# Two units of eight products instead of four ahead of the first block's seven-product units, and a place of its own for one token sum of the second block

## The chip, the cores and the metric

The kernel runs on one core of one Trainium2 chip. The metric is the device time of one execution in microseconds (us), the median of three runs.

## What is computed

A decoder trunk of one layer over 16 meta tokens and 512 real tokens, width 1024: a gated feed-forward block, a token mixer (two kinds of attention with gated branches), and a second gated feed-forward block. Cut to what the change touches:

```python
def swiglu(h, w_in, w_out):
    gu = h @ w_in
    gate, up = jnp.split(gu, 2, axis=-1)
    return (jax.nn.silu(gate) * up) @ w_out

h = h + 0.5 * swiglu(rms_norm(h, ffn1_norm[l]), ffn1_w_in[l], ffn1_w_out[l])
h = h + token_mixer(rms_norm(h, mix_norm[l]), ...)
h = h + 0.5 * swiglu(rms_norm(h, ffn2_norm[l]), ffn2_w_in[l], ffn2_w_out[l])
```

D_FF is 2816, so `w_in` has 2 x 22 column groups of 128: 22 **units** `u`, each a gate group and an up group.

## The kernel before, in words

Every matrix product is made of float32 operands split into a high part (`hi`, L130, a cast on ScalarE, called ACT in the rows) and a rest (`lo`, L137 or L139, a subtraction on VectorE, DVE); a product of 128 features is three matmuls on TensorE, PE (L275, L276, L278 in `prod`).

**Two kinds of unit.** The features of the input (1024) are halved into 2 x 512 and the tokens into two halves, which gives blocks A11, A12 (first token half) and A21, A22. A *plain* unit (`Units.plain`) makes all eight block products: per gate and up, two token halves and two feature halves, each 4 x 3 = 12 matmuls, 96 in all. A *seven* unit (`Units.seven`, called by `Units.unit`) takes gate and up together as a 2 x 2 block product by Winograd's form with seven products, 84 matmuls, out of A11, A12, A22 and four token sums S1 to S4 (`Halves.sums`, built by `Halves.diff`, L398, and split by `parts`).

**Weights.** A plain unit takes two pieces of 128x1024, each loaded with one DMA (L236) and split once. A seven unit takes four pieces, A, B, C and D: A is landed in two halves on the queue of SyncE, SP (L191), and a third DMA adds to its second half while it lands (`add`, L195, issued on the queue of GpSimd, POOL); C is landed and added to in the same way, D is landed; B is made of C and D by two additions on DVE (L217, L218) in a tile `tc`, of which there is one. A, B and C are split at 1024 columns, D at 512 into a tile `wD`. There are three buffers each for `raw`, `wh` and `wl`, two each for `rawC` and `rawD`. `piece()` hands out a piece, splits up to three ahead and loads up to five ahead.

**Order.** `NC = (4, 3)` is the number of plain units with which the first and the second block begin. `ffn_pieces` lists the weights accordingly, and `early` weaves the steps of the plain units with the entry of the second token half and the four token sums; the loops after it run the seven units from `NC` on. In the first block the entry belongs to this: `enter_first` and `enter_rest` bring in the tokens (squares on ACT, `entry_rms` on DVE, then a power operation on POOL, L319, in `rsq`; then `entry_scale` on DVE, L623), and `enter_second` transposes the second token half on PE (L631) and splits A21 and A22. The plain units need all four blocks.

The program's text does not fix the order on the engines: a planner orders the instructions of each engine by its own estimate of when their operands are there, and lets a later one go ahead where an earlier one is not ready; only where the code asks for it (`issue_after`, `inline`) is the order kept. Each engine and each queue then works strictly in that order, and an instruction that waits holds up all behind it. A DMA issued on POOL waits on POOL's queue like any other instruction.

In the second block the sums S3, S1, S2 and S4 get their places from `places2` (in this order: `tc`, `own`, `tc`, and `own` again), and `acts_tile2(1)` is the tile for the activations of units 2 and 3.

Of the kernel before, what the change touches and what calls it, by code (L numbers as in the profile page):

```python
# [11 lines left out]
F32 = mybir.dt.float32  # L12
# [22 lines left out]
KG1 = [(0, 4), (4, 3), (7, 4)]  # L35
KG2 = [(0, 4), (4, 4), (8, 3)]
NU = DFF // P
NC = (4, 3)
TH = T // 2


# [38 lines left out]
def kernel(  # L80
# [32 lines left out]
    def nm(s):  # L113
        nid[0] += 1
        return f"{s}_{nid[0]}"
# [35 lines left out]
    def ffn_pieces(wi, wo, second):  # L151
        nc_ = NC[second]
        for j0, n in KG2 if second else KG1:
            for i, u in enumerate(in_turns(j0, n)):
                if 2 * j0 + i < nc_:
                    pieces.extend([("w", [(wi[u], 8, 128)]), ("w", [(wi[NU + u], 8, 128)])])
                else:
                    seven_pieces(wi[u], wi[NU + u], 4)
            if second:
                for m in range(0, KD, 2):  # L160
                    cut = lambda m: wo[m // 4][:, 2 * j0 : 2 * (j0 + n), P * (m % 4) : P * (m % 4) + P]
                    seven_pieces(cut(m), cut(m + 1), n)
            else:
                for m in range(0, KD, 2):
                    seven_pieces(*(wo[m + b][:, 2 * j0 : 2 * (j0 + n)] for b in range(2)), n)
# [573 lines left out]
    def early(X, ff, dsts, second, sums, more, alone=0):  # L739


        u = [ff.plain(d, i == 0 and not alone) for i, d in enumerate(dsts)]
        main = u[0][:4] + u[1][:2]
        if alone:
            main[1:1] = [enter_rest]
        run(main[:alone] + second[:3] + main[alone:] + second[3:] if alone else weave(main, second))
        run(weave(u[0][4:] + [s for v in ([u[1][2:]] + u[2:]) for s in v], sums + more))
# [96 lines left out]
    ]  # L844
    early(X, ff1, [act1(u) for u in range(NC[0])], second, X.sums(), [nothing], 6)
    def rest_of(m):

        hi(xH[:, m], hT[:, m], gmT[:, m : m + 1])
        lo(xL[:, m], hT[:, m], xH[:, m], gmT[:, m : m + 1])
        if m == 0:  # L850
            A.activation(sqacc, hT[:, m], AF.Square)
        else:
            sq = ff1.new("u", 2, 2)
            A.activation(sq, hT[:, m], AF.Square)
            (V if m > 5 else G).tensor_tensor(out=sqacc, in0=sqacc, in1=sq, op=ALU.add)
        A.dma_start(h1d[:, m], hT[:, m, M:])
        G.tensor_copy(xm[:, m, 0:M], xH[:, m, :M].bitcast(F32))
        i = G.tensor_copy(xm[:, m, 32 : 32 + M], xL[:, m, :M].bitcast(F32))
        shared["xm"] = getattr(i, "ins", i)
# [22 lines left out]
    for gi, (j0, n) in enumerate(KG1):  # L882
        for u in range(max(2 * j0, NC[0]), 2 * (j0 + n)):
            does = (lambda f, *v: lambda: [f(i) for i in v])
# [652 lines left out]
    for hf in range(2):  # L1537
        c = slice(S // 2 * hf, S // 2 * (hf + 1))
# [20 lines left out]
    def acts_tile2(i):  # L1559

        if i == 2:
            t = kp.tile([P, KD, S], F32, tag="o", name=nm("acts2")).bitcast(F32R).rearrange("p k c -> p (k c)")
        else:
            t = ap2.tile([P, 7 * S], F32R, tag=f"acts{i}", name=nm("acts2"), bufs=1)
        return t[:, : 7 * S].rearrange("p (b a c) -> p b a c", b=2, a=7)

    def places2():
        own = ap2.tile([P, 2 * S], F32, tag="own", name="own", bufs=1)
        new_tc = lambda: ap2.tile([P, PW], F32, tag="tc", name=nm("tc"), bufs=1)
        return [new_tc, lambda: own, new_tc]  # L1570

    X2.new_places = places2
    X2.a21 = lambda: acts_tile2(3)
# [9 lines left out]
    ]  # L1583
    early(X2, ff2, [act2(u) for u in range(NC[1])], second, [nothing] + X2.sums(), [])
    stage = {}
# [17 lines left out]
    for gi, (j0, n) in enumerate(KG2):  # L1603
        for u in range(max(2 * j0, NC[1]), 2 * (j0 + n)):
            ff2.unit(act2(u), u == 2 * (j0 + n) - 1)
# [77 lines left out]
```

## Time and profile before

| | us |
|---|---|
| median of three runs | 1091.29 (1090.96 to 1091.56) |
| the profiled execution | 1090.99 |
| its span, first to last instruction | 1089.2 |
| PE busy in the span | 1079.7 |
| DVE busy | 851.2 |
| ACT busy | 612.6 |
| POOL busy | 177.5 |

Of the profiled execution 1090.99 - 1089.2 = 1.8 us lie around the span. A busy share is a mean over stages with different limits. PE's matmuls are pipelined, so that what one costs is read from the distance between two starts, not from its own duration.

### The profile page before, as it was taken

What the parts mean: (1) busy time and instruction counts of PE and PEld (TensorE: products, weight loads), DVE (VectorE), ACT (ScalarE), POOL (GpSimd) and SP (SyncE); (2) the same over time, 40 slices, a digit from 0 to 9 for tenths busy, and PEclk for the clock granted to TensorE, in tenths of its full rate; (3) what the DMA queues carried; (4) which work ended last, traced back from release to release, by engine and by line L of the source; (5) the groups of instructions that cost most, each with busy time, mean ns of one, the idle gap of its engine ahead of it and who ended that gap; (6) DMA issues with size and microseconds to landing.
All of it is one profiled execution on the core that took longest, in us unless ns stands there. A gap on an engine that the chain in (4) does not pass through costs nothing.

```text
span 1089.2 us, 21633 instructions
## 1 busy us (share of the span) xinstructions
PE 1079.7 (99%) x8407; PEld 1035.8 (95%) x8407; DVE 851.2 (78%) x1616; ACT 612.6 (56%) x1143; POOL 177.5 (16%) x209
## 2 busy tenths in 40 slices
PE   8999999999999999999999999999999999999998
PEld 7999999999999999999887888899999999999998
DVE  7868868988889577788787655578898778887895
ACT  7556456656666455456555633355476466645664
POOL 1011111112124431122100000000122211221120
PEclk9999999999999999999999999999999999999999
DMA  8478787688776323112211224456588877887753
GB/s 274 128 192 190 179 197 197 151 220 215 178 178 172 120 81 117 57 42 80 79 59 58 78 78 138 153 180 188 141 198 178 201 188 180 177 199 186 166 123 102
DMA packets 107111, 163.84 MB, mean 150 GB/s; under 512 B 10288, under 2 KB 57648, under 8 KB 107008
## 3 DMA queue, kind: packets, MB, share of 16 engines
q1 hardware_dynamic: 71440, 119.67, 34.6%
q0 software_dynamic: 25888, 31.02, 19.2%
q10 hardware_dynamic: 9680, 11.77, 3.4%
q8 instruction: 66, 1.08, 0.4%
q14 instruction: 37, 0.30, 0.1%
HBM read 158.19 MB, written 6.32 MB: 151 GB/s over the span
## 4 chain that ended last, share of the span: by engine, by line
PE 90%; DVE 5%; ACT 2%; DMA 2%; issue 1%; POOL 0%; ACTq 0%; SPq 0%; DVEq 0%
PE ps L275 15%; PE ps L276 15%; PE ps L278 15%; PE pt L275 12%; PE pt L276 12%; PE pt L278 12%; DVE wl L137 1%; DMA raw<-in_w2i_dram 1%; ACT wh L130 1%; ACT t L1140 1%; PE pt L1225 0%; PE pt L1180 0%; DMA raw<-in_w1i_dram 0%; DMA xt<-in_x_dram 0%; PE ps L1347 0%
## 5 line engine op out<-in xcount | busy, mean ns | idle before, releaser
L276 PE MATMUL ps<-x,wh 128*128 128x264 f32 (+2 forms) x768 | 224.6, 293 | 0.8 <-DVE x L139 0.4
L275 PE MATMUL ps<-x,wh 128*128 128x264 f32 (+2 forms) x768 | 225.1, 293 | 0.1
L278 PE MATMUL ps<-x,wl 128*128 128x264 f32 (+2 forms) x768 | 224.1, 292 | 0.0
L130 ACT CAST wh<-raw 128x1024 fp32r<-128x1024 f32 (+3 forms) x134 | 137.8, 1030 | 125.7 <-PE ps L276 50.1
L137 DVE TENSOR_TENSOR wl<-raw,wh 128x1024 fp32r<-128x1024 f32 (+3 forms) x134 | 161.1, 1203 | 54.1 <-ACT wh L130 51.4
L276 PEld LDWEIGHTS ps<-x,wh 128*128 128x128 f32 x768 | 144.6, 188 | 3.7 <-DVE x L139 0.9
L275 PEld LDWEIGHTS ps<-x,wh 128*128 128x128 f32 x768 | 144.8, 189 | 3.3 <-ACT hT L650 0.3
L278 PEld LDWEIGHTS ps<-x,wl 128*128 128x128 f32 x768 | 144.7, 188 | 2.8
L275 PE MATMUL pt<-x,wh 128*128 128x264 f32 (+2 forms) x416 | 125.4, 301 | 0.0
L276 PE MATMUL pt<-x,wh 128*128 128x264 f32 (+2 forms) x416 | 124.9, 300 | 0.0
L278 PE MATMUL pt<-x,wl 128*128 128x264 f32 (+2 forms) x416 | 124.6, 300 | 0.0
L275 PE MATMUL ps<-acts,wh 128*128 128x264 f32 (+1 forms) x352 | 100.4, 285 | 0.1
L278 PE MATMUL ps<-acts,wl 128*128 128x264 f32 (+1 forms) x352 | 99.6, 283 | 0.0
L276 PE MATMUL ps<-acts,wh 128*128 128x264 f32 (+1 forms) x352 | 99.5, 283 | 0.0
L137 DVE TENSOR_TENSOR wl<-tc,wh 128x1024 fp32r<-128x1024 f32 (+1 forms) x61 | 72.4, 1188 | 33.1 <-ACT wh L130 32.9
L130 ACT CAST wh<-tc 128x1024 fp32r<-128x1024 f32 (+1 forms) x61 | 62.3, 1021 | 58.7 <-DVE tc L218 47.2
L278 PEld LDWEIGHTS pt<-x,wl 128*128 128x128 f32 x416 | 78.5, 189 | 2.8
L275 PEld LDWEIGHTS pt<-x,wh 128*128 128x128 f32 x416 | 78.4, 188 | 2.9 <-issue 0.3
L276 PEld LDWEIGHTS pt<-x,wh 128*128 128x128 f32 x416 | 78.2, 188 | 2.5
L137 DVE TENSOR_TENSOR wl<-rawC,wh 128x1024 fp32r<-128x1024 f32 (+1 forms) x61 | 73.1, 1199 | 5.7 <-ACT wh L130 5.4
L130 ACT CAST wh<-rawC 128x1024 fp32r<-128x1024 f32 (+1 forms) x61 | 62.2, 1020 | 25.5 <-PE pt L276 19.2
L275 PEld LDWEIGHTS ps<-acts,wh 128*128 128x128 f32 x352 | 66.4, 189 | 0.7 <-DVE h2T L877 0.3
(368 smaller groups left out, 3065.8 us busy)
## 6 DMA issues: line engine op xcount, KB each, us to landing
rawC<-in_w2i_dram SPq DMA_DIRECT2D x19, 512.0 KB, 4.4
raw<-in_w2i_dram SPq DMA_DIRECT2D x38, 256.0 KB, 3.3
rawC<-in_w1i_dram SPq DMA_DIRECT2D x18, 512.0 KB, 4.5
raw<-in_w1i_dram SPq DMA_DIRECT2D x36, 256.0 KB, 3.4
raw<-in_wm_dram SPq DMA_DIRECT2D x18, 512.0 KB, 4.5
raw<-in_wg_dram SPq DMA_DIRECT2D x16, 512.0 KB, 3.4
raw<-in_wout_dram SPq DMA_DIRECT2D x16, 512.0 KB, 3.4
rawD<-in_w2i_dram SPq DMA_DIRECT2D x19, 256.0 KB, 3.8
```

The costliest lines, as they stand in the source:

```text
L130: return A.copy(o, i)
L137: return V.tensor_tensor(out=o, in0=i, in1=h, op=ALU.subtract)
L275: PE.matmul(ps, sH, mH, start=first, stop=False, **more)
L276: PE.matmul(ps, sH, mL, start=False, stop=False, **more)
L278: shared["mm"] = PE.matmul(ps, sL, mH, start=False, stop=last, **more)
L1140: A.activation(t, t, AF.Exp, bias=nmx, scale=-1.0, accum_out=l[:, j : j + 1])
```

## The change

`NC` becomes (2, 3): units 2 and 3 of the first block are seven units. Their weights are loaded and combined like those of the other seven units, and the token sums are woven into two plain units. In the second block the third sum to be built, S2, no longer gets the shared tile `tc` but the first 1024 float32 columns of the tile for the activations of units 2 and 3.

```diff
-NC = (4, 3)
+NC = (2, 3)
...
     def places2():
         own = ap2.tile([P, 2 * S], F32, tag="own", name="own", bufs=1)
         new_tc = lambda: ap2.tile([P, PW], F32, tag="tc", name=nm("tc"), bufs=1)
-        return [new_tc, lambda: own, new_tc]
+
+        pair = acts_tile2(1).rearrange("p b a c -> p (b a c)").bitcast(F32)
+        return [new_tc, lambda: own, lambda: pair]
```

## Rows read from the trace of the kernel before

**Rows 1.** The page's head: busy us of the engines, share of the span, instructions.
```profile
PE 1079.7 (99%) x8407; PEld 1035.8 (95%) x8407; DVE 851.2 (78%) x1616; ACT 612.6 (56%) x1143; POOL 177.5 (16%) x209
```
**Rows 2.** Busy time by stretch: us, PE, PEld, DVE, ACT, POOL, clock, DMA share, GB/s.
```profile
25.50:40.20 14.70, 14.70 (x121) 14.70 (x121) 14.37 (x19) 9.21 (x16) 0.00 (x0) 1.00 0.28 95
40.20:51.90 11.70, 11.70 (x98) 11.70 (x97) 8.59 (x14) 5.16 (x9) 1.74 (x2) 1.00 0.55 136
51.90:63.60 11.70, 11.70 (x98) 11.70 (x97) 5.38 (x8) 3.19 (x5) 1.70 (x2) 1.00 0.67 161
```
**Rows 3.** PE in order of time: the first matmuls of units 2, 3 and 4.
```profile
40.23 0.28 PE L275 MATMUL ps<-x,wh 128*128 128x264 f32 x1
...
51.93 0.29 PE L275 MATMUL ps<-x,wh 128*128 128x264 f32 x1
...
63.60 0.28 PE L275 MATMUL ps<-x,wh 128*128 128x264 f32 x1
```
**Rows 4.** DVE in order of time: splits of S2 and S4, first addition of B.
```profile
40.28 1.25 DVE L137 TENSOR_TENSOR x<-acts,x 128x1056 fp32r<-128x1056 f32 x1
...
44.23 1.25 DVE L137 TENSOR_TENSOR x<-acts,x 128x1056 fp32r<-128x1056 f32 x1
...
54.62 0.69 DVE L217 TENSOR_TENSOR tc<-rawC,rawD 128x512 f32<-128x512 f32 x1
```
**Rows 5.** POOL in order of time, 15 to 20 us.
```profile
15.48 1.05 POOL L195 DMA_DIRECT2D rawC<-in_w1i_dram  x1 [6.29 <-DMA rawC<-in_w1i_dram]
16.72 0.87 POOL L195 DMA_DIRECT2D rawC<-in_w1i_dram  x1 [0.19 <-issue]
19.39 0.71 POOL L319 TENSOR_TENSOR rin<-rin,nhalf 128x2 f32<-128x2 f32 x1 [1.80 <-DVE rin L613]
```
**Rows 6.** SP's queue in order of time: issues at 7 and 15 us.
```profile
7.09 1.34 SPq L191 DMA_DIRECT2D rawC<-in_w1i_dram  x2
...
15.08 0.33 SPq L236 DMA_DIRECT2D raw<-in_w1i_dram  x1
```
**Rows 7.** Tile `raw`, 15.0 to 15.2 us: landing of the issue at 15.08.
```profile
DMA to landing us min/median/max: 5.3/5.3/5.3
```
**Rows 8.** Tile `raw`, 17.0 to 17.3 us: landing of the issue at 17.17.
```profile
DMA to landing us min/median/max: 7.0/7.0/7.0
```
**Rows 9.** Tile `raw`, 0 to 70 us: shortest, median and longest landing.
```profile
DMA to landing us min/median/max: 2.6/4.4/8.7
```
**Rows 10.** DVE, then PE, in order of time, 13 to 21 us.
```profile
13.82 1.23 DVE L137 TENSOR_TENSOR wl<-raw,wh 128x1024 fp32r<-128x1024 f32 x1
...
15.92 1.22 DVE L137 TENSOR_TENSOR wl<-raw,wh 128x1024 fp32r<-128x1024 f32 x1
...
19.13 0.17 DVE L613 TENSOR_SCALAR rin<-rin 128x2 f32<-128x2 f32 x1 [0.76 <-ACT sq L598]
20.14 1.42 DVE L623 TENSOR_SCALAR xt<-xt,rin 128x1024 f32<-128x1024 f32 x2 [0.83 <-DMA raw<-in_w1i_dram]
...
21.04 0.30 PE L631 MATMUL pt<-ident,xt 128*128 128x128 f32 x1 [0.63 <-DVE xt L623]
```
**Rows 11.** Second block, DVE in order of time: split of B, S2, S4.
```profile
779.67 1.23 DVE L137 TENSOR_TENSOR wl<-tc,wh 128x1024 fp32r<-128x1024 f32 x1 [0.53 <-ACT wh L130]
780.93 1.23 DVE L398 TENSOR_TENSOR tc<-own,x 128x1024 f32<-128x1024 f32 x1
...
783.54 1.22 DVE L137 TENSOR_TENSOR x<-tc,x 128x1024 fp32r<-128x1024 f32 x1
```
**Rows 12.** Second block, PE in order of time, and the stretch around it.
```profile
784.25 0.28 PE L276 MATMUL pt<-x,wh 128*128 128x256 f32 x1
784.82 0.38 PE L276 MATMUL ps<-x,wh 128*128 128x256 f32 x1 [0.28 <-DVE x L137]
...
780.00:790.00 10.00, 9.72 (x83) 9.52 (x82) 9.93 (x13) 6.19 (x11) 0.79 (x1) 1.00 0.42 95
```

## What the change was predicted to do

> **What bounds the kernel now.** I read the page's head first, then the busy time by stretch, then PE, DVE, POOL and SP in order of time. PE is busy in 1079.7 of 1089.2 us [rows 1], and in the stretch that the change touches it never rests: from 25.50 us (first product with the second token half) to 63.60 (first seven unit) all of every stretch is PE time [rows 2]. So a matmul that is left out there is worth its full distance, as long as PE's operands keep coming. DVE is the engine to watch: 14.37 of 14.70 us in the stretch up to 40.20, then 8.59 and 5.38 of 11.70 while units 2 and 3 run plain [rows 2]. Before 25 us PE does rest: at 21.04 it has waited 0.63 us for the scaled second token half, which DVE could scale only at 20.14, after POOL's power operation from 19.39 to 20.10 [rows 5, 10]. That chain (ACT's squares, DVE at 19.13, POOL, DVE, PE) has no slack at all.
>
> **Fewer matmuls.** A plain unit is 96 matmuls: units 2 and 3 start at 40.23 and 51.93, unit 4 at 63.60, so 11.7 us each and 0.122 us a matmul [rows 3]. A seven unit is 84. Two units x 12 matmuls x 0.122 = **-2.92 us**, all of it on the path.
>
> **More work on DVE, and earlier.** Per unit a plain one splits two pieces of 1.22 us [rows 10], 2.4 us; a seven unit splits three of them and D (half the columns, about 0.7), and adds C and D in two steps of 0.69 [rows 4], 5.7 us in all: 3.3 more, 6.6 for two units. In the 23.4 us of units 2 and 3 DVE is idle 23.4 - 8.59 - 5.38 = 9.4 us [rows 2]; the stretch shrinks by 2.9 and takes 6.6 more, 9.5. So the cover is just used up. The sums themselves come in time even in the present order: S2 is split at 41.5 and S4 at 45.5 [rows 4], and a first seven unit that starts at 40.2 wants S2 as its third product (2.9 us in, 43.1) and S4 as its seventh (8.8 us in, 49.0). The order would have to slip 1.4 us (the two additions of B) to touch S2. With three buffers a split is made some two pieces ahead, so a late DVE is felt only after some us. Bounds: 0, and 2 us if the slip and the late splits add up; the nearest row is the second block's same passage, where DVE is 9.93 of 10 us busy and PE loses 0.28 [rows 12]. I take **+0.3**. That DVE gains by having fewer plain steps is excluded, since its work only grows.
>
> **More DMA, and where its queue goes.** Two units load 1.75 MB each in place of 1 (A 512 KB and 256 added, C 512 and 256 added, D 256: seven times 256 KB against four). The DMA share in the stretches is 0.28, 0.55 and 0.67 [rows 2], so bytes are no bound there, taken at 0. The place where they are issued is another matter. Unit 2's A now takes the buffer that a plain piece had: its landing is issued at 15.08, the moment the second piece's split ends (13.82 + 1.23) [rows 6, 10], and the third DMA, the one that adds, goes to POOL's queue and waits there. Behind it, or ahead of it, stands the power operation of 19.39 on which enter_second depends. Who is first is the planner's choice by its own estimate. The trace has a hint: the two additions to rawC belong to units 4 and 5, far later in the program's text than the power operation, were issued by SP at 7.09 and stand ahead of it at 15.48 and 16.72; the first held POOL 6.29 us until its data had landed [rows 5, 6]. So the planner lets an addition go first when it thinks that it is ready first. From the landing's issue at 15.08 to the power operation there are 4.3 us; that is close to a landing time here. If the addition is first: A's two halves are the 512 KB of the piece that landed 5.3 us after its issue, at 20.4 [rows 6, 7]; the addition's issue takes 0.87 to 1.05 [rows 5], so the power operation begins at 21.4, 2.0 us late, and DVE's scale, PE's transposes and all the dense stretch behind move by as much. Queued behind the waiting addition on POOL is only this power operation; waiting for that are DVE's two scales, then PE's transposes. Bounds: with the shortest landing, 2.6 [rows 9], A's second half (issued 0.33 later) is there at 18.0 and the addition is done by 19.0, cost 0; with 7.0 us, the next issue's landing [rows 8], 23.4, cost 4.0. I take the row of the transfer in the very same place, **+2.0**.
>
> The Trainium skill ("DMA: Bandwidth & Descriptors", section "Anatomy of one DMA") fits a transfer to 2.0 us and its bytes at 436 GB/s. For 256 KB that is an estimate of 2.6 us, by which the addition would be gone before 19.39 whatever the order, and the sum would be that of the first rival. The trace disagrees here: the landing took 5.3 us, in a queue that was full [rows 7].
>
> **The second block's sum.** S2 gets `tc` only when B has been split out of it: B's split runs to 780.90, S2 is built at 780.93 and split from 783.54 to 784.76, and PE's two matmuls at 784.25 and 784.82 are 0.57 us apart where 0.12 is usual [rows 11, 12]. With its own place S2 can be built right after S1, some 20 us earlier. That gives back **-0.45 us**; what is late next is B's own split, two pieces ahead, so nothing. The tile it borrows is first wanted by unit 2's activations at its end, and they then wait for S4, which reads S2; S4 moves forward with S2, so I take 0, between 0 and the 0.45 that is gained.
>
> **Sum.** -2.92 + 0.3 + 2.0 - 0.45 = -1.07. The profiled execution is 1090.99 (span 1089.2 and 1.8 around it), so 1089.9; the median of the runs is 0.30 above it, so **1090.2 us**.
>
> **The rivals.**
> 1. *The power operation goes first, or A lands in time.* Then the term of 2.0 is gone: -3.07, **1088.2**. For it: the margin that the planner sees is not in the trace, and the shortest landing [rows 9] would do. Against it: the additions to rawC [rows 5].
> 2. *Slower: unit 3's A goes first as well.* It is landed into the third buffer, free at 17.14 [rows 10]; the piece that went there landed after 7.0 us, at 24.2 [rows 8]. Its addition would hold POOL to 25.2, the power operation would start 5.8 us late, and the sum is -2.92 + 0.3 - 0.45 + 5.8 = +2.7, **1094.0**. It decides from the point where the planner puts a landing at under 2.2 us (17.17 to 19.39), which is short against its apparent treatment of the others; the change loses outright from a delay of 3.1 us on.
> 3. *DVE becomes the bound of the passage*, with 2 us in place of 0.3, on top of the late power operation: +0.6, **1091.9**. For it: the cover is used up to 0.1 us [rows 2]. Against it: the lead of two pieces.
>
> That the change does not do what it says is no case of its own: the count of matmuls follows from the text.
>
> **How the numbers follow.** Forecast 0.45, rival 1 0.32, rival 2 0.12, rival 3 0.11. A measurement can tell about 0.2%, 2.2 us, from no change. Faster by more: rival 1 and a tenth of the forecast (a delay under 0.9 us), 0.36. Slower by more: rival 2 and the far end of the forecast and of rival 3, 0.14. Within: 0.50. The range runs from rival 1 less a little (no stall in the passage, 1087.9) to rival 3 and the forecast's upper bound of 4.0 us (1092.2), so 1087.8 to 1092.4; rival 2 is left out.
>
> **What would show it.** PE's matmuls are 24 fewer; unit 4's first product comes 2.9 us earlier relative to the first product at 25.50. POOL's queue has an L195 on `raw` ahead of the power operation that stood at 19.39, and PE's wait at 21.04 grows from 0.63 to about 2.6. PE's rest at 784.8 is gone and the L398 for S2 stands near 765. Right after unit 1, DVE is near 10 of 10 us and PE loses a few tenths. The prediction is wrong if the power operation keeps its time (then it is rival 1), or if PE rests for more than 1 us in units 2 and 3.

## The result and the profile after

The changed kernel takes **1094.25 us** (median, 1092.43 to 1097.29) against 1091.56 us of the kernel before in the same comparison; the ratio is **1.0023, 95% interval 1.0016 to 1.0030**. It is slower by about 2.5 us where 1.1 us less had been forecast, and it lies outside the range. The profiled execution took 1093.92 us with a span of 1091.5, 2.3 us more than the span before. The accounts below are made on these two spans. The medians differ by 2.7 us; some 0.4 of it lies outside the span, where no view shows it: the time less the span is 1.7 to 1.9 us in all executions of the kernel before that list both, and 1.7 to 4.9, with a median of 2.4, in the changed kernel.

I read the page's head first. It answers [rows 1].

```profile
PE 1079.0 (99%) x8383; PEld 1035.3 (95%) x8383; DVE 858.1 (79%) x1628; ACT 619.2 (57%) x1155; POOL 180.9 (17%) x213
```

24 matmuls fewer, as forecast, and yet PE's busy time is only 0.7 us smaller instead of 2.9. So PE worked more slowly somewhere, besides resting more.

**POOL, 15 to 23 us**, in order of time (start, duration, engine, line, operation, out<-in, idle time before it and what ended that); this answers [rows 5].

```profile
15.34 1.05 POOL L195 DMA_DIRECT2D rawC<-in_w1i_dram  x1 [6.22 <-DMA rawC<-in_w1i_dram]
18.68 0.88 POOL L195 DMA_DIRECT2D rawC<-in_w1i_dram  x1 [2.29 <-DMA rawC<-in_w1i_dram]
21.71 0.84 POOL L195 DMA_DIRECT2D raw<-in_w1i_dram  x1 [2.15 <-issue]
22.27 1.02 POOL L319 TENSOR_TENSOR rin<-rin,nhalf 128x2 f32<-128x2 f32 x1
```

The addition to `raw`, unit 2's A, stands ahead of the power operation, which is now at 22.27 instead of 19.39, 2.88 us later. The profile names no releaser for the 2.15 us that POOL waited ahead of this addition ("issue"); what fits is the landing of A's second half, issued at 15.63, which comes 0.53 us ahead of it.

Tile `raw`, 15.6 to 15.7 us, landing:
```profile
DMA to landing us min/median/max: 5.6/5.6/5.6
```

**DVE, 19 to 25 us**, in order of time; this and the next answer [rows 10].

```profile
19.31 0.17 DVE L613 TENSOR_SCALAR rin<-rin 128x2 f32<-128x2 f32 x1 [0.76 <-ACT sq L598]
...
23.32 1.42 DVE L623 TENSOR_SCALAR xt<-xt,rin 128x1024 f32<-128x1024 f32 x2 [3.31 <-POOL rin L319]
```

**PE, 20 to 30 us**, in order of time; its first product with the second half, at 29.53, was at 25.50 [rows 2].

```profile
20.66 0.28 PE L275 MATMUL ps<-x,wh 128*128 128x264 f32 x1
24.22 0.45 PE L631 MATMUL pt<-ident,xt 128*128 128x128 f32 x1 [3.29 <-DVE xt L623]
24.46 0.42 PE L631 MATMUL ps<-ident,xt 128*128 128x128 f32 x1
...
27.41 0.37 PE L276 MATMUL ps<-x,wh 128*128 128x264 f32 x1
...
29.53 0.39 PE L275 MATMUL pt<-acts,wh 128*128 128x264 f32 x1
```

DVE has the sum of squares at 19.31, hardly later than before, and then waits for POOL. PE rests 3.29 us where it rested 0.63. And behind that rest its transposes start 0.21 to 0.24 us apart; in the kernel before they were 0.11 apart:

```profile
21.17 0.27 PE L631 MATMUL ps<-ident,xt 128*128 128x128 f32 x1
21.28 0.27 PE L631 MATMUL pt<-ident,xt 128*128 128x128 f32 x1
...
23.03 0.37 PE L276 MATMUL ps<-x,wh 128*128 128x264 f32 x1
...
25.50 0.39 PE L275 MATMUL pt<-acts,wh 128*128 128x264 f32 x1
```

The busy time of the changed kernel by stretch (us, PE, PEld, DVE, ACT, POOL, clock, DMA share, GB/s) says why:

```profile
23.00:24.00 1.00, 0.00 (x0) 0.00 (x0) 0.68 (x2) 0.00 (x0) 0.29 (x1) 0.94 0.90 141
24.00:25.00 1.00, 0.78 (x4) 0.81 (x5) 1.00 (x3) 0.00 (x0) 0.22 (x1) 0.50 0.78 137
...
27.00:28.00 1.00, 1.00 (x10) 1.00 (x9) 0.94 (x3) 1.00 (x5) 0.00 (x0) 0.86 1.02 180
```

The granted clock falls to 0.50, 1.2 in place of 2.4 GHz, at the end of the rest and comes back between 27 and 28 us. The transposes and what lies between them take 27.41 - 24.22 = 3.19 us; before, the same from 21.04 to 23.03 took 1.99.

**The passage into the seven units**, PE in order of time: the first matmuls of unit 2 and of unit 4 (first and last line) and the two around a stall; this answers [rows 3], where unit 2 began at 40.23 and unit 4 at 63.60.

```profile
44.26 0.28 PE L275 MATMUL ps<-x,wh 128*128 128x264 f32 x1
...
47.06 0.28 PE L278 MATMUL ps<-x,wl 128*128 128x264 f32 x1
48.31 0.39 PE L275 MATMUL ps<-x,wh 128*128 128x264 f32 x1 [0.97 <-ACT pt L496]
...
65.93 0.28 PE L275 MATMUL ps<-x,wh 128*128 128x264 f32 x1
```

The busy time of the stretch (columns as above):

```profile
44.26:54.50 10.24, 9.27 (x77) 9.06 (x76) 10.21 (x15) 6.56 (x13) 0.29 (x1) 1.00 0.79 213
```

From 25.50 to unit 2 it was 14.73 us, from 29.53 to 44.26 it is 14.73 again: the two plain units are untouched. Then PE is held 1.25 us between two matmuls that are 0.12 apart elsewhere. It waits for ACT's copy of the unit's first product (L496). ACT in order of time:

```profile
43.42 1.08 ACT L130 CAST x<-acts 128x1056 fp32r<-128x1056 f32 x1 [0.45 <-DVE acts L398]
45.43 1.08 ACT L130 CAST x<-acts 128x1056 fp32r<-128x1056 f32 x1 [0.93 <-DVE acts L398]
46.41 0.63 ACT L130 CAST acts<-u 128x528 fp32r<-128x528 f32 x1
46.94 1.04 ACT L130 CAST wh<-rawC 128x1024 fp32r<-128x1024 f32 x1
...
47.89 0.37 ACT L496 COPY pt<-ps 128x264 f32<-128x264 f32 x1
```

The copy is queued behind the high parts of S2 (43.42) and S4 (45.43), a cast of activations and the cast of C. S4's cast waits 0.93 us for DVE, which in this stretch is busy 10.21 of 10.24 us.

**The second block.** S2 in its new place, then split, both on DVE, far ahead of their use; these answer [rows 11].

```profile
769.09 1.22 DVE L398 TENSOR_TENSOR acts<-own,x 128x1024 f32<-128x1024 f32 x1
...
773.19 1.22 DVE L137 TENSOR_TENSOR x<-acts,x 128x1024 fp32r<-128x1024 f32 x1
```

PE's rest at the third product [rows 12] is gone. But look at PE in order of time, the 2500th and the 500th matmul from the end. In the kernel before:

```profile
787.86 0.28 PE L276 MATMUL pt<-x,wh 128*128 128x256 f32 x1
...
1024.81 0.28 PE L275 MATMUL ps<-x,wh 128*128 128x256 f32 x1
```

And in the changed one:

```profile
790.25 0.28 PE L276 MATMUL pt<-x,wh 128*128 128x256 f32 x1
...
1027.53 0.28 PE L275 MATMUL ps<-x,wh 128*128 128x256 f32 x1
```

The same 2000 matmuls take 236.95 us before and 237.28 after, without a rest in either. What the rest gives back is spent there.

**How late the changed kernel is, place by place**, by the same matmul in both traces: at the first product with the second half +4.03 (29.53 - 25.50); at unit 4 +2.33 (65.93 - 63.60); at the 2823rd matmul from the end, just ahead of the second block, +2.75; at the 2500th +2.39, since the rest is gone; at the 500th +2.72; at the end of the span +2.32, mostly since the last wait for the output is 0.3 shorter (PE waited 0.75 us for ACT's copy of the output before, and 0.46 after). The loss is made before 30 us and partly paid back by the seven units; the rest of the program moves it by 0.4 us at most in either direction.

### The profile page after: what moved, and what is told of

Same layout as the page of the kernel before. It is cut to its first block, busy times and chain, and to the rows that moved or that the text cites. A ratio compares the mean times of both kernels' runs of the same rounds, so it can differ in the third digit from the quotient of the medians.

```text
span 1091.5 us, 21619 instructions
## 1 busy us (share of the span) xinstructions
PE 1079.0 (99%) x8383; PEld 1035.3 (95%) x8383; DVE 858.1 (79%) x1628; ACT 619.2 (57%) x1155; POOL 180.9 (17%) x213
## 4 chain that ended last, share of the span: by engine, by line
PE 93%; DVE 3%; ACT 3%; issue 1%; POOL 0%; ACTq 0%; DVEq 0%; POOLq 0%
PE ps L275 16%; PE ps L276 15%; PE ps L278 15%; PE pt L275 13%; PE pt L276 13%; PE pt L278 13%; ACT wh L130 1%; DVE wl L137 1%; PE ps L313 1%; ACT t L1140 1%; PE pt L1180 1%; PE pt L1225 0%; PE ps L1347 0%; PE pt L1347 0%; DVE t L1143 0%
## 5 line engine op out<-in xcount | busy, mean ns | idle before, releaser
L130 ACT CAST wh<-raw 128x1024 fp32r<-128x1024 f32 (+2 forms) x132 | 135.7, 1030 | 120.5 <-PE ps L276 49.0
L137 DVE TENSOR_TENSOR wl<-raw,wh 128x1024 fp32r<-128x1024 f32 (+2 forms) x132 | 158.6, 1202 | 49.0 <-ACT wh L130 47.8
L137 DVE TENSOR_TENSOR wl<-tc,wh 128x1024 fp32r<-128x1024 f32 (+1 forms) x63 | 74.9, 1189 | 31.4 <-ACT wh L130 31.3
L130 ACT CAST wh<-tc 128x1024 fp32r<-128x1024 f32 (+1 forms) x63 | 64.4, 1023 | 55.2 <-DVE tc L218 48.7
L137 DVE TENSOR_TENSOR wl<-rawC,wh 128x1024 fp32r<-128x1024 f32 (+1 forms) x63 | 75.6, 1199 | 5.7 <-ACT wh L130 5.4
L130 ACT CAST wh<-rawC 128x1024 fp32r<-128x1024 f32 (+1 forms) x63 | 64.3, 1021 | 23.3 <-PE pt L276 17.8
```

Source lines behind the costliest of these rows:

```text
L130: return A.copy(o, i)
L137: return V.tensor_tensor(out=o, in0=i, in1=h, op=ALU.subtract)
```

## The experiments

Each ratio is against the kernel before in the same comparison. The theory from the trace of the changed kernel: the delay is POOL's order (the addition ahead of the power operation, which holds it up: the hold, below), made larger by the clock behind the long rest, and a second loss comes from ACT's order at the passage. The rivals: that DVE's load is the price; that the units themselves gain less than their matmuls; that the second block's new place costs what it gives.

**1. The power operation first.** In the changed kernel the addition of A is made to be issued after the power operation, and one piece fewer is loaded at the very beginning, so that the addition does not come up before it.

```diff
-        add(raw[:, 128 * n :], b2[:, n:])
+        with tc.issue_after(shared["pow"]):
+            add(raw[:, 128 * n :], b2[:, n:])
...
-        load_to(c + 5)
+        load_to(c + 5 if c else 4)
...
```


> The changed kernel, with unit 2's A loaded one piece later and its addition queued on POOL behind the power operation. Theory 1 (the held power operation and the low clock after it are the loss): PE waits about 0.6 us for the second token half in place of 3.3, the granted clock stays at 1.0, the first product with that half begins near 25.6 us in place of 29.5, and the time is 4.0 us under the changed kernel, 1.3 to 1.5 under the kernel before (ratio 0.9987). Rival (DVE is the bound of the passage): PE starts earlier but then waits for DVE's or ACT's results in units 2 and 3, and at most 1 us comes back (ratio 1.0014 or more).

Measured 1089.26 us, ratio **0.9980 (0.9971 to 0.9988)**. This edit, the order of two instructions on POOL's queue with a load one piece later, turns the change from a loss of 0.23% into a gain of 0.2%; DVE and PE have the same number of instructions in both. POOL in order of time:

```profile
21.43 0.71 POOL L320 TENSOR_TENSOR rin<-rin,nhalf 128x2 f32<-128x2 f32 x1 [1.00 <-DVE rin L615]
22.11 0.95 POOL L195 DMA_DIRECT2D raw<-in_w1i_dram  x1
```

ACT at the passage, in order of time:

```profile
44.34 0.36 ACT L498 COPY pt<-ps 128x264 f32<-128x264 f32 x1 [0.54 <-PE ps L279]
...
45.17 1.08 ACT L130 CAST x<-acts 128x1056 fp32r<-128x1056 f32 x1 [0.47 <-DVE acts L400]
```

The power operation now waits for DVE alone. With the other times the planner also put ACT's copy ahead of S4's cast, and the stall of 1.25 us at the passage is gone; some 0.4 us are lost at 48.7 us in its place. So this run removed both losses, and the two have to be told apart by others. (In this profiled execution the clock was at half from 12.8 to 19.6 us, which is why everything in it is late: the first product with the second half comes at 27.90, not near 25.6 as had been expected. See the last section.)

**2 and 3. The clock.** Matmuls on the identity, into the bank that the transposes overwrite, fill PE's wait ahead of them; POOL's order is left as it is.

```diff
+        if hf and ks[0] == 0:
+            with after(shared["mm"]):
+                for _ in range(26):
+                    PE.matmul(pss[0][:, :P], ident, ident, start=True, stop=True)
```


> The changed kernel, with 26 matmuls of no use on PE (the identity by itself) ahead of the transposes of the second token half; the addition still stands ahead of the power operation. Theory 1 splits the 4.0 us lost there into some 2.7 of waiting and 1.2 of transposes at half clock: the power operation stays near 22.3 us, the transposes still begin near 24.2, but at 0.11 us each in place of 0.21 and at granted clock 1.0, so that 1.2 to 1.4 us come back (ratio 1.0011). Rival (the transposes are slow for another reason, or what follows waits for DVE anyway): ratio stays at 1.0023.

Measured 1094.48 us, ratio 1.0021 (1.0011 to 1.0031): nothing gained, but the size was wrong. 26 of them last 5.7 us, to 26.3 us, so that PE was still at them when the operands had come; the first product with the second half came at 30.89. The second run has 14:

> As e2_filled_wait with 14 matmuls of no use in place of 26: each is two PE instructions of 0.11 us, so that the 26 lasted 5.7 us and overran the wait of 3.3; 14 last 3.1. Theory 1: the transposes begin near 24.2 at granted clock 1.0 and 0.11 us each, the first product with the second token half near 28.2 us in place of 29.5, and 1.2 to 1.4 us come back (ratio 1.0011). Rival (the clock costs nothing of its own): ratio 1.0023 as the changed kernel.

Measured 1093.19 us, ratio **1.0011 (1.0002 to 1.0019)**. PE in order of time:

```profile
24.14 0.33 PE L635 MATMUL pt<-ident,xt 128*128 128x128 f32 x1 [0.40 <-DVE xt L623]
24.30 0.27 PE L635 MATMUL ps<-ident,xt 128*128 128x128 f32 x1
...
26.33 0.37 PE L275 MATMUL ps<-x,wh 128*128 128x264 f32 x1
...
28.96 0.39 PE L275 MATMUL pt<-acts,wh 128*128 128x264 f32 x1
```

The stretches (columns as above):

```profile
20.00:24.00 4.00, 3.74 (x34) 3.54 (x32) 0.85 (x2) 0.23 (x1) 1.58 (x2) 1.00 0.99 226
24.00:28.00 4.00, 3.83 (x29) 3.22 (x29) 3.85 (x10) 2.72 (x9) 0.90 (x1) 1.00 0.72 115
```

The transposes start as late as in the changed kernel (24.14 against 24.22), but with the clock at 1.00, 0.11 us apart from the second on. From the first transpose to the product behind the last it is 26.33 - 24.14 = 2.19 us in place of 3.19, so 1.00 us less at the full clock. But the first product with the second half comes at 28.96, only 0.57 earlier than in the changed kernel and not near 28.2: four matmuls which PE does ahead of its wait there stand behind the transposes here, 0.5 us.

The ratio is 0.0012 lower, 1.3 us. In the traces it is 1.1 us, of which one half is this 0.57 and the other the stall at the passage, 0.75 us here instead of 1.25. That 1.3 is near the 1.2 us of the slow transposes is therefore chance. The intervals of the two ratios just overlap; what the clock costs, 1.0 to 1.2 us, is read from the traces and not from the times. One of the 17 executions of the changed kernel lists a mean clock of 1.000 over its span, the others 0.994 to 0.998; its span of 1089.9 us is the shortest (the others 1090.7 to 1093.2). No trace of it was kept, so whether its wait was shorter too is not known.

**4. The copy in ACT's queue.** The power operation first, and the cast of C pinned behind the copy in the first seven unit.

```diff
...
-            w = piece()
+            first = state["use"] == 2 * NC[0]
+            w = piece(2 if first else None)
...
-            A.copy(a[:, :th], b[:, :th])
+            i = A.copy(a[:, :th], b[:, :th])
+            if first:
+                shared["copy"] = state["use"] + 1, getattr(i, "ins", i)
```


> As e1_power_first, and in the first seven unit ACT's copy of the first product stands ahead of the cast of C. Theory 1: of the 1.1 us that PE waits there in the changed kernel, some 0.8 is ACT's order and comes back beyond e1_power_first (ratio 0.9980); the rest waits for the split of S2. Rival: PE waits for S2's or B's split on DVE just as long, and e1_power_first and this one take the same time (ratio 0.9987).

Measured 1091.23 us, ratio 0.9996 (0.9987 to 1.0005): worse than the first experiment, a miss. The pin moved the casts of S4 and of the activations ahead of the copy instead. PE in order of time:

```profile
44.67 0.28 PE L284 MATMUL ps<-x,wl 128*128 128x264 f32 x1
46.88 0.39 PE L281 MATMUL ps<-x,wh 128*128 128x264 f32 x1 [1.93 <-ACT pt L504]
```

ACT in order of time:

```profile
44.41 1.07 ACT L130 CAST x<-acts 128x1056 fp32r<-128x1056 f32 x1 [2.96 <-DVE acts L405]
...
46.46 0.37 ACT L504 COPY pt<-ps 128x264 f32<-128x264 f32 x1
```

PE is held 2.21 us, behind a cast for which ACT had waited 2.96 us. With the copy ahead of S4's cast (experiment 1) nothing is lost at this place; here it is 2.1 us, and this kernel is 2.0 us slower than that one (1091.23 and 1089.26). In the two traces the passage as a whole costs 1.8 us more here, of which shorter waits later give 0.4 back. It is the copy's place in ACT's queue that sets the price of the passage.

**5. Three plain units.** `NC = (3, 3)`, else the changed kernel. One unit's gain, half the seven units' work on DVE, and another moment at which A is loaded.

> The changed kernel with three plain units in the first block. Unit 3's A is loaded later than unit 2's was, so that its addition stands behind the power operation. Theory 1: no wait over 0.7 us and no low clock at the transposes, one unit of 12 matmuls fewer (1.46 us) and the 0.45 us of the second block: 1.9 us under the kernel before (ratio 0.9983), or less by what PE waits for in the shorter passage. Rival (a seven unit that early costs more than it saves, whatever POOL does): not under the kernel before (ratio 1.000 or more).

Measured 1091.04 us, ratio 0.9991 (0.9982 to 1.0000). POOL:

```profile
19.71 0.71 POOL L319 TENSOR_TENSOR rin<-rin,nhalf 128x2 f32<-128x2 f32 x1 [2.13 <-DVE rin L613]
```

Here the planner left the addition of A behind the power operation by itself, PE's rest ahead of the transposes was 0.65 us (0.63 in the kernel before) and the clock stayed at 1.00. Of the unit's 1.46 us the median shows 0.6, and the trace's span is 0.7 shorter (1088.5 against 1089.2): no large loss where there is no hold, but half the gain is missing. By the same matmul in both traces this kernel is 0.33 us late at the first product with the second half (25.83 and 25.50), 1.11 early at 68 us, as the unit's 1.46 less the 0.33 would have it, and only 0.38 early just ahead of the second block. So 0.7 us go in small steps between 68 and 749 us; why is not shown.

**6. Power operation first, and two plain units in the second block too.** `NC = (2, 2)` on top of experiment 1.

> As e1_power_first, and the second block too begins with two plain units. Theory 1: 12 matmuls fewer, another 1.4 us under e1_power_first if PE does not wait in the second passage (ratio 0.9967). Rival: DVE is full there (9.9 of 10 us in the kernel before), PE waits for splits or copies and it is no faster than e1_power_first (ratio 0.9980 or more).

Measured **1088.50 us, ratio 0.9967 (0.9955 to 0.9979)**, faster than both kernels. POOL in order of time:

```profile
19.72 0.95 POOL L320 TENSOR_TENSOR rin<-rin,nhalf 128x2 f32<-128x2 f32 x1
```

PE's waits from 740 to 800 us (us in total, times, longest):

```profile
PE ps L338 <- POOL r L320: 0.6, 1, 0.6
```

The first product with the second half is at 26.07, 0.57 us later than before, not 4.03. The second block's own power operation has become a short wait there, 0.6 us: an addition to `raw` (747.49) stands just ahead of it (748.16), which the edit does not prevent. Whether the second block's unit gave its 1.4 us is not shown. The intervals of this run and of experiment 1 overlap, and from just ahead of the second block to the 2500th matmul from the end it is 38.68 us here and 38.92 there, 0.24 less for 12 matmuls fewer.

**7. More of the hold.** The changed kernel with the additions of units 2 and 3 both ahead of the power operation: a measured dose of the suspected cause, and the second rival of the prediction made real.

```diff
...
-        load_to(c + 5)
+        load_to(c + 5 if c else 9)
...
-        rsq(rin[:, c], rin[:, c])
+        with tc.issue_after(shared["add"]) if a == 3 else ExitStack():
+            rsq(rin[:, c], rin[:, c])
```


> The changed kernel with the additions of both unit 2's and unit 3's half of A ahead of the power op on POOL's queue. If the hold at the second halves goes into the time one to one: the third addition lands near 24.5 us (one landing of 2.6 to 3 us behind the 22.3 at which the second is done), the power op starts near 25.4, TensorE's transposes near 27.3 at the half clock, so the first product with the second half comes some 3 us later than in the changed kernel: ratio 1.0050. Rival, that the lag of the first units is taken up later, where VectorE is the bound of the passage: ratio 1.0023, as the changed kernel.

On the same chip the changed kernel itself, once more:

> The changed kernel itself, unchanged, as the base for the two other runs on this chip: ratio 1.0023 as in its first measurement.

Measured: 1096.10 us, ratio **1.0033 (1.0020 to 1.0046)**, and the changed kernel 1094.50 us, ratio **1.0018 (1.0010 to 1.0027)**. POOL of the dosed kernel, in order of time:

```profile
25.37 0.86 POOL L195 DMA_DIRECT2D raw<-in_w1i_dram  x1 [2.32 <-DMA raw<-in_w1i_dram]
25.93 1.03 POOL L320 TENSOR_TENSOR rin<-rin,nhalf 128x2 f32<-128x2 f32 x1
```

PE, where the transposes begin:

```profile
27.90 0.45 PE L633 MATMUL pt<-ident,xt 128*128 128x128 f32 x1 [5.65 <-DVE xt L625]
```

The instructions stand near where they were expected, half a microsecond late; the first product with the second half comes at 32.43, 2.2 us later than in the changed kernel's trace of this comparison (30.21) and 2.9 later than in the first (29.53). The spans of the two traces differ by 1.9 us (1094.2 and 1092.3): the 2.2, less 0.3 by which the later waits for ACT's copies together are shorter. The medians differ by 1.6 us. The expectation of 3 us was too high, since the changed kernel's own hold was 0.7 us longer in this comparison than in its first trace; but what is added to the hold goes into the time, and little of it (0.3 of 2.2 us) is taken up later, where the rival had all of it. The two intervals overlap, so this rests on the traces more than on the times.

**8 and 9. The two parts of the change alone.** First the new place for S2 alone, with `NC = (4, 3)`:

> The kernel before with only the new place of S2 in the second block. Theory 1: PE's rest at 784.8 us goes and 0.45 us come back (ratio 0.9996). Rival: the rest goes, but the matmuls behind it take 0.1 to 0.2% longer than in the kernel before, as the changed kernel's profile and three others show (59.3 us in place of 59.2 for 500 of them), and the time is the same within 0.1 us (ratio 1.0000).

Measured 1091.89 us, ratio 1.0003 (0.9994 to 1.0011): no gain. In its trace the rest at the third product is gone too, and the 2000 matmuls take 237.21 us. Then the two units alone, with S2 in its old place:

> The changed kernel with S2's old place: only the two units are changed. Theory 1: the loss is all in the first 50 us, the second block's rest is back and the time is 0.45 us over the changed kernel (ratio 1.0027). Rival as in e6_place_alone: the same time as the changed kernel (ratio 1.0023), and 500 matmuls of the second block take 59.2 us.

Measured 1092.81 us, ratio 1.0010 (0.9999 to 1.0021), with times from 1090.46 to 1095.35, far apart for one kernel: not conclusive. Its profiled execution had the clock at half between 12 and 19 us, the mean being 0.57 (columns as above):

```profile
12.00:20.00 8.00, 7.76 (x38) 7.07 (x38) 6.84 (x13) 6.97 (x15) 1.80 (x2) 0.57 1.01 360
20.00:24.00 4.00, 4.00 (x36) 4.00 (x35) 2.31 (x6) 1.59 (x4) 1.71 (x3) 1.00 0.97 217
```

POOL in order of time:

```profile
20.74 0.84 POOL L195 DMA_DIRECT2D raw<-in_w1i_dram  x1 [0.61 <-DVE hT L652]
21.30 1.02 POOL L319 TENSOR_TENSOR rin<-rin,nhalf 128x2 f32<-128x2 f32 x1
```

There DVE had the sum of squares only at 20.83 (19.31 in the changed kernel). A had landed by then, so that the addition, still ahead of the power operation, held it by 0.2 us only. PE was late too, with products of the first half until 23.3 us; it did not rest, and the clock did not fall again. The first product with the second half came at 27.46, 2.07 us earlier than in the changed kernel: the hold is a race between the landing and the sum of squares, and here the loss that lay ahead covered it. Once more, on the chip of the dose:

> The two units alone, the second block's third token sum in its old place, once more, now beside the changed kernel itself on one chip. If the new place is worth nothing, the two have the same ratio, 1.0023 each; if it is worth its wait of 0.56 us, this one is 0.0005 higher.

Measured 1095.09 us, ratio 1.0022 (1.0010 to 1.0034), beside 1.0018 for the changed kernel: no difference that the two intervals, each some 1.0 to 1.3 us to either side, can tell. In the two traces the new place wins 0.18 us up to the 2500th matmul from the end and loses 0.45 over the 2000 behind it.

**10. The place asked for, but not used.**

```diff
-        return [new_tc, lambda: own, new_tc]
+        reserve = lambda: (acts_tile2(1), new_tc())[1]
+        return [new_tc, lambda: own, reserve]
```


> The kernel before with one thing done: the tile for the activations of units 2 and 3 is asked for where the changed kernel asks for it, when the third sum gets its place, but the sum itself stays in the shared tile. Nothing is computed otherwise or in another order. If the matmuls that read activations are longer because these tiles come to lie elsewhere in the memory, the rest of 0.56 us at the third product stays and the 2000 matmuls from the 2500th to the 500th from the end take 237.2 us in place of 236.95: ratio 1.0003, to be read from the trace, since the time can't tell it. Rival, that it is the sum in that tile or the order of work around it: 236.9 us and ratio 1.0000.

Measured 1091.55 us, ratio 0.9993 (0.9983 to 1.0003); the 2000 matmuls take 236.96 us, as in the kernel before. So asking for the tile at the third sum does not make the matmuls longer. But that is not quite where the changed kernel asks for it, other than the expectation says: there the request stands in `places2` itself, which runs when the first sum, S3, gets its place. A request as early as that was not tried without the sum in it, so where these tiles come to lie in the memory is not ruled out as the cause.

## Why the prediction was wrong, step by step

**Fewer matmuls, -2.92: right.** 8383 instead of 8407. From unit 2 to unit 4 it is 65.93 - 44.26 = 21.67 us against 23.37 before, 1.70 less, and with the 1.13 lost at the stall 2.83.

**The power operation, +2.0: the right mechanism, mis-sized; it cost 4.0.** That the addition would stand ahead of it was chosen against the first rival, and it does. Two terms were too small. The wait: A's second half was issued at 15.63 and landed at 21.18, 5.6 us after its issue, 0.8 later than the 20.4 that I took from the landing of the piece that had been there; the power operation came at 22.27 in place of 21.4, and took 1.02 us instead of 0.71, so that the transposes began 24.22 - 21.04 = 3.18 us later. And what I did not have at all: PE's clock. I let everything behind the wait "move by as much", as if 3 us of rest changed nothing for the work that follows. The transposes took 1.20 us more at half clock. Three matmuls that now stood ahead of the wait took back 0.35: 3.18 + 1.20 - 0.35 = 4.03. The upper bound of 4.0 that I gave for this term from the 7.0 us landing was met by two causes, of which one was missing: that it fits is luck.

The Trainium skill ("DMA: Bandwidth & Descriptors", "Anatomy of one DMA") gives its fit for the path of GpSimd's DMAs. A's halves are issued by SyncE, so the prediction's estimate of 2.6 us was carried over to another path, and the 5.3 us set against it there were those of a piece of 512 KB; this landing of 256 KB took 5.6 us. On GpSimd's own queue the fit is too short here as well: the 20 additions of 256 KB to `raw` in this block took 4.7 us to land, by the median.

**The passage, +0.3: the wrong queue, and too little; it cost 1.13, and 0.4 more later.** I counted DVE's work against its idle time and concluded that PE would lose a few tenths. DVE is indeed full, 10.21 of 10.24 us, and yet PE waited for none of its splits. It waited for a copy on ACT, which the planner had queued behind a cast that waited for DVE. The step that failed is "a late DVE is felt only after some us": it reached PE at once, through ACT's queue. Two more copies of the same kind are late at 113.9 and 363 us (0.33 and 0.19 more than before; at unit 4 to the end of the first block the lateness grows from 2.33 to about 2.7). That is near the third rival's 2 us in size, but not by its mechanism.

**S2's place, -0.45: the rest went, the time did not.** 0.36 us were won ahead of the 2500th matmul from the end (2.75 to 2.39) and 0.33 lost over the 2000 behind it. Over all runs, the ten traces of kernels with the new place need 237.16 to 237.34 us for these 2000 matmuls, and the four with the old place 236.87 to 236.96. In the one pair that differs in nothing but the place (the second run of experiment 9 and the changed kernel beside it) the whole difference of 0.45 us lies in the 672 matmuls that read activations, 118.5 ns each in the old place and 119.2 in the new (118.8 in the kernel before); those that read tokens are equal to 0.1 ns. Why is open; a request for the tile at the third sum alone does not do it (experiment 10). I had not asked what else a borrowed place could change.

**The sum.** In the two traces it is 4.03 - 2.83 + 1.13 + 0.42 - 0.36 + 0.33 - 0.40 (the end) = 2.32, the difference of the spans. The 1094.25 has 0.27 more since the kernel before took 1091.56 in this comparison and not 1091.29, and some 0.4 that lie outside the span. The second rival gave 1094.0, but that this is near is luck, since its cause was not there: unit 3's addition stands behind the power operation, at 24.78. Made real in experiment 7, it is slower still. What the first rival stated, that without the hold the change would bring 3.1 us, is near what experiment 1 showed, 2.4 us (1089.26 against 1091.64).

So the order was read rightly and the kernel is faster with the other one. The range was too narrow because the bound of 4.0 for the hold was added to a passage at 0.3 or 2 us, never both at their ends (together they give 1093.9), and the chance of slower (0.14) hung almost wholly on the second rival.

## What to carry to other kernels

Here an accumulating DMA on POOL's queue made that queue wait until the data it adds to had landed (2.15 us for A's in the changed kernel); before bringing such a load forward, list what small instruction stands behind it and who waits for that, and pin the small one first. A wait of TensorE is not priced by its length alone: ask what the clock does behind it, and add the slower work that follows. And where an engine becomes full, look at the others' queues for instructions that wait for it with something urgent behind them: here the stall came out there, not on the full engine.

## What the runs showed of the hardware

TensorE's granted clock fell to 0.50 within a rest of 3.3 us (20.9 to 24.2 us), at 23.9, and stayed there until 27.3 us. With the rest of 0.63 us before, and with one of 1.93 us in experiment 4, it stayed at 1.00; with 5.65 us of rest (experiment 7) it was at 0.50 from 24.5 to 31.4 us. Matmuls on the identity in the wait kept it at 1.00.

In some executions the clock is at half early, within 12 to 20 us: it is so in four of the thirteen traces of changed and tried kernels (0.57 to 0.79 on the mean of 12 to 20 us), while two executions of the very same program (experiment 9) differ in it. In the 4 us ahead of it PE was busy 2.84 to 3.20 us in these four, with no rest over 0.7 us; the kernel of experiment 10, busy 2.77 us from 8.5 to 12.5, kept 1.00. What decides it no run here shows. The Trainium skill ("TensorE: Matmul & The Clock Gate", "Part 1: The HAM clock gate") says that how many matmuls at the start run at the low clock differs from one execution of a kernel to the next; that is another place than this one, which lies some 10 us behind the first matmul.

The kernel before seems to have it too: in the comparison of experiment 7, 12 of its 23 executions list a mean clock of 0.997 or 0.998, and their median span is 1090.8 us against 1089.5 for the others. That would account for the changed kernel's ratio of 1.0018 there and 1.0023 in the first comparison, but without traces of these executions it is not shown. Nor is it shown for the spread of the kernels with a hold (1090.46 to 1095.35 us in experiment 9); the one trace of such an execution, read there, shows the hold gone.

That a matmul takes 118.5 or 119.2 ns from start to start with a tile's place lent out or not, over hundreds of them, was not expected either, and is not explained.
